# A planned schedule with larger GpSimd costs, margins for side matmuls, and parameters loaded with x

## The chip, the cores and the metric

One core of one Trainium2 chip. The metric is device time in microseconds: 293.01 us before the change (median of three runs, 292.58 to 294.14).

## The reference, cut to what matters

Two layers over 256 tokens of width 1024, all in float32. Each layer normalises the stream, projects it once, splits the result over three groups of heads, gates each, joins them and projects back:

```python
for l in range(DEPTH):                                   # DEPTH = 2
    u = rms_norm(x, g_pre[l]) @ w_in[l]
    (qa, ka, va, ga, qb, kb, vb, gb, rb, qm, gm) = jnp.split(u, split_idx, axis=-1)
    oa = moba_attention(norm(qa), norm(ka), va) * silu(ga)          # 8 heads, causal, ALiBi
    log_a = log_sigmoid(rb @ w_gate_up[l] + b_gate_up[l]) / 16
    ob = rms_norm(gla_attention(qb, kb, vb, log_a)) * silu(gb)      # 4 heads, gated linear, chunks of 64
    mk, mv = jnp.split(rms_norm(mem, g_mem[l]) @ w_mem_kv[l], 2, axis=-1)
    om = mem_attention(norm(qm), norm(mk), mv) * silu(gm)           # 4 heads into 256 memory tokens
    x = x + jnp.concatenate([oa, ob, om], axis=-1) @ w_out[l]
```

## The kernel before, in words

**Projections.** The stream lies transposed on chip (`xT`, eight k blocks of 128 x 256). Weights come in granules of 1024 x 256, 1 MB each, on SyncE's queue into three buffers (`raw`). To multiply float32 exactly enough, every operand is split into a high and a low part: ScalarE copies to the high part (`whi`, L380), VectorE subtracts for the low part (`wlo`, L382), and each product is three matmuls (L974; L981 where two granules are done side by side with 512 columns). A layer has 19 granules, 48 matmuls each; they are issued by `main()` in the order of `UNITS`, the granule gb and four output granules o0 to o3 last. The first output granule goes over k in the order of `KORD` (6, 7, 1, 0, 2, ...), two matmul groups per k. These are the projections; all the other matmuls are called side matmuls here: sums of squares (L414), the row form of the scale (L431), transposes of the normalised heads (L478), the low-rank gate (L499, L506), gated linear attention (L655 to L723), attention scores (L856), transposes of the probabilities (L908) and their product with the values (L923). Those of 64, 32 or 16 rows or columns are "tiled".

**Other engines.** GpSimd does the powers of -1/2 for the norms (L421 with 2, L458 with 8 elements a partition), the scaling of the probabilities (L893), copies of q with the heads kept apart (L534), and a share of the copies for which the planner may choose (L249: `xh`, `oh`, `zl`, `qsh`). L465 applies the norm to the heads, L708 is the product of gated linear attention, fed by copies into `att`. `put_o` (L826, L828) splits a finished head pair for the output projection.

**The planner.** No engine's order is written out by hand. Everything is a generator that yields operations to `Plan`, each with an engine (or several to choose from), a cost in nanoseconds and a time at which its inputs are ready. `Plan.run` picks again and again the operation that can start first, on the alternative that ends first; among operations of that engine that could start by then the highest priority goes. It writes the instruction there and books the engine. Projections have priority 0, side work 5 to 10. So costs and ready times decide the order of instructions and who does a copy; the hardware then runs each engine's queue in that order, waiting on semaphores. `begin` adds the cost of changing TensorE between full and tiled shape (`ENTER`, `LEAVE`, `CROSS`). `LANDS` are the planned landing times of the first chunks. GpSimd's costs: `gcost` for scaled copies and powers written in place:

```python
def gcost(n, scalar=False):
    return 330 + 0.83 * n if scalar else 75 + 2.42 * n
...
t1 = yield op("G", 800, t, 9)
G.tensor_tensor(r, v, nhalf[:, 0:2], op=ALU.pow)
...
t = yield op("G", 1620, t, prio)
G.tensor_tensor(c, ss, nhalf, op=ALU.pow)
```

**The start.** `start_loads` sends the parameters (`prm`: gains and biases, 46 floats a partition, 23 KB) on ScalarE's queue first, then an activation that brings in the exp table, then the first two weight chunks of kq; x, the first granule vr and the rest of kq go on SyncE's queue in five steps of k. The first scaling of x (L247) needs x and the parameters.

Of the kernel before, what the change touches and what calls it, by code (L numbers as in the profile page):

```python
# [16 lines left out]
P = 128  # L17
L = 2
KT = 8
T = 256  # L20
EPS = 1e-6
NPRM = 23
# [8 lines left out]
MEMPRIO = 6  # L31
WARM = 6
CHUNKS = ((0, 1), (1, 2), (2, 4), (4, 6), (6, 8))
LANDS = ((3400, 4800, 5300), (5300, 5700, 5800), (6600, 7200, 7900), (8600, 9300, 10000), (10600, 11300, 12000))
ENTER, LEAVE, CROSS = 89.0, 189.0, 60.0
C_ID = 0
C_MASK = 128
C_DIAG = 128 + 80
# [4 lines left out]
class Plan:  # L43
# [10 lines left out]
    def spawn(self, gen, prio=0):  # L54
        self.ready.append(Task(gen, prio))

    def begin(self, t, eng):
        s = max(t.after, self.free[eng])
        if eng == "P" and t.mode != self.shape:
            s += ENTER if self.shape == "full" else LEAVE if t.mode == "full" else CROSS  # L60
        return s

    def run(self):
        while True:
            while self.ready:
                self.step(self.ready.pop(0))
            if not self.pending:
                return
            best, pick = None, {}
            for t in self.pending:  # L70
                s, eng, cost = min(((self.begin(t, e), e, c) for e, c in t.alts), key=lambda a: a[0] + a[2])
                pick[t] = (s, eng, cost)
                key = (s, -t.prio, t.seq)
                if best is None or key < best[0]:
                    best = (key, eng)
            s, eng = best[0][0], best[1]
            t = min((t for t in self.pending if pick[t][1] == eng and max(t.after, self.free[eng]) <= s),
                    key=lambda t: (-t.prio, t.seq))
            s, _, cost = pick[t]
            self.pending.remove(t)  # L80
            if t.table and t.table != self.table:
                self.table = t.table
                cost += 1283.0
            self.free[eng] = s + cost
            if eng == "P":
                self.shape = t.mode
            t.value = s + cost + self.LAT[eng]
            if len(t.alts) > 1:
                t.value = (eng, t.value)
            self.step(t)  # L90
# [64 lines left out]


@with_exitstack
def trunk(ctx, tc, xT_d, memT_d, wvr_d, win_d, wmkv_d, wout_d, prm_d, wup_d, cst_d, nb_d, out_d):
    nc = tc.nc
    cp = ctx.enter_context(tc.tile_pool(name="cp", bufs=1))  # L160
    sp = ctx.enter_context(tc.tile_pool(name="sp", bufs=1))
# [9 lines left out]
    def big(shape, nm, dt=F32, parts=P):  # L171
        return cp.tile([parts] + shape, dt, name=nm)
# [4 lines left out]
    def ev():  # L177
        return Event(plan)

    xT = big([KT, T], "xT")  # L180
    xh, xl = big([KT, T], "xh", F32R), big([KT, T], "xl", F32R)
    oh, ol = big([KT, T], "oh", F32R), big([KT, T], "ol", F32R)
    prm, cst = big([L, NPRM], "prm"), big([N_CONST], "cst")
    wup = big([L, P], "wup", parts=16)
    nb = big([8, T], "nb")
    ident = cst[:, C_ID:C_ID + P]
# [46 lines left out]
        return (55 if psum else 95) + 0.83 * n + 93 * ptr  # L233

    def gcost(n, scalar=False):
        return 330 + 0.83 * n if scalar else 75 + 2.42 * n

    def copy(dst, src, n, psum, after, prio=None, scale=None, alts="SV"):
        costs = {"S": scost(n, psum, 0 if scale is None else 1),
# [66 lines left out]
        return t  # L306

    def start_loads():
        prm_t = 3550
        S.dma_start(prm, prm_d)  # L310
        S.activation(warm, ones, AF.Exp)
        tiles = []
        for i in range(2):
            l, nm, src, n = seq[i]
            got, t0 = yield ("acq", raws, 1)
            raw, src = sub(got[0][2], n), src.rearrange("p (k n) -> p k n", n=n)
            ts = [ev() for _ in range(KT)]
            tiles.append((raw, src, ts))
            plan.spawn(split(i, l, nm, n, got, ts, CHUNKS), 6)
        for (a, b), (tx, tv, tq) in zip(CHUNKS, LANDS):  # L320
            nc.sync.dma_start(xT[:, a:b], xT_d[:, a:b])
            plan.spawn(first_x(a, b, max(tx, prm_t)), 9)
            for (raw, src, ts), tw, q in zip(tiles, (tv, tq), (nc.sync, nc.scalar if b <= 2 else nc.sync)):
                q.dma_start(raw[:, a:b], src[:, a:b])
                for k in range(a, b):
                    ts[k].set(tw)
        plan.spawn(first_sq(tx), 5)
        nc.sync.dma_start(cst, cst_d)
        cst_ev.set(12300)
        nc.sync.dma_start(wup, wup_d)  # L330
# [78 lines left out]
    def stats(sq, t, out, Rout):  # L409
        got, t0 = yield ("acq", banks, 1)  # L410
        ps = got[0][2]
        t = yield op("P", 300, max(t, t0), 9)
        for tt in range(2):
            TE.matmul(ps[:, tt:tt + 1], lhsT=sq[0][2][:, tt * P:tt * P + P], rhs=ones, start=True, stop=True)  # L414
        sqsp.release(sq, t)
        v, e, r = (small([2], n) for n in ("vx", "evx", "rsx"))
        t = yield op("V", 80, t, 9)
        V.tensor_scalar(v, ps[:, 0:2], 1.0 / 1024, EPS, op0=ALU.mult, op1=ALU.add)
        banks.release(got, t)
        t1 = yield op("G", 800, t, 9)  # L420
        G.tensor_tensor(r, v, nhalf[:, 0:2], op=ALU.pow)  # L421
        t = yield op("V", 80, t, 9)
        V.tensor_scalar(e, v, EPS, None, op0=ALU.mult)
        out.set(t1, (r, e))
        if Rout is not None:
            got, t0 = yield ("acq", banks, 1)
            tc_ = yield ("wait", cst_ev)
            ps = got[0][2]
            t = yield op("P", 430, max(t1, t0, tc_), 9)
            for tt in range(2):  # L430
                TE.matmul(ps[:, tt * P:tt * P + P], lhsT=r[:, tt:tt + 1].to_broadcast([P, P]), rhs=ident,  # L431
                          start=True, stop=True)
            t = yield op("V", vcost(T), t, 9)
            V.tensor_copy(R_t, ps[:, :T])
            banks.release(got, t)
            Rout.set(t)

    def headnorm(parts, e, after_read, prio=None):
        got, t0 = yield ("acq", sqp, 1)
        sq = got[0][2]  # L440
        t = t0
        for ps, a, t1 in parts:
            n = ps.shape[1]
            t2 = yield op("S", scost(n * T, True), max(t1, t0), prio)
            S.activation(sq[:, a:a + n], ps, AF.Square, scale=0.125)
            t = max(t, t2)
        ss, c = small([8], "ss"), small([8], "cc")
        t = yield op("V", vcost(512), t, prio)
        V.tensor_reduce(ss, sq.rearrange("p t (h d) -> p (t h) d", d=64), axis=AX, op=ALU.add)
        sqp.release(got, t)  # L450
        t = yield op("V", 90, t, prio)
        if e is None:
            V.tensor_scalar(ss, ss, EPS, None, op0=ALU.add)
        else:
            s2 = ss.rearrange("p (t h) -> p t h", t=2)
            V.tensor_tensor(s2, s2, e[:, :, None].to_broadcast([P, 2, 4]), op=ALU.add)  # L456
        t = yield op("G", 1620, t, prio)
        G.tensor_tensor(c, ss, nhalf, op=ALU.pow)  # L458
        got, t0 = yield ("acq", nhp, 1)
        t = max(t, t0)  # L460
        for ps, a, _ in parts:
            n = ps.shape[1]
            v = ps.rearrange("p t (h d) -> p (t h) d", d=64)
            t = yield op("V", vcost(n * T), t, prio)
            V.tensor_tensor(got[0][2][:, a:a + n].rearrange("p t (h d) -> p (t h) d", d=64), v,  # L465
                            c[:, 4 * a:4 * a + 4 * n, None].to_broadcast([P, 4 * n, 64]), op=ALU.mult)
        after_read(t)
        return got, t
# [537 lines left out]
            wrel[l, nm][k // 2].set(t)  # L1006

    def main():
        yield op("P", 5400)
        for j in range(WARM):  # L1010
            TE.matmul(banks.slots[7][2][:, 0:256], lhsT=zero[:, 0:128], rhs=zero, start=True, stop=True)
        idx = {(l, n): i for i, (l, n, _, _) in enumerate(seq)}
        for l in range(L):
# [5 lines left out]
            for unit in UNITS[l] if l == 0 else ("vr", "kq", *UNITS[l]):  # L1019
# [15 lines left out]
                for k, m in order:  # L1035
# [3 lines left out]
                        tw = max(tw, tx)  # L1039
                    tx = yield ("wait", aev[k])  # L1040
                    if len(names) == 2:
                        t = yield op("P", 680, max(tb, tw, tx))
                        mms2(bk[m][2].rearrange("p (a n) -> p a n", a=2), act, k, m, k == 0, k == KT - 1)
                    else:
                        t = yield op("P", 360 * n / 256, max(tb, tw, tx))
                        ps = bk[m][2][:, :n] if nbk == 2 else bk[0][2][:, m * T:m * T + T]
                        mms(ps, l, kind, done[l, nm], act, k, m, k == 0, k == KT - 1)
                    ends[m] = t
# [28 lines left out]
            for g in range(4):  # L1077
# [16 lines left out]
                for k, m in order:  # L1094
                    tw = yield ("wait", wts[l, nm][k])
                    to = yield ("wait", oev[l][k])
                    w = done[l, nm]
                    t = yield op("P", 360, max(tb, tw, to))
                    ps = bk[m][2][:, :T]
                    mms(ps, l, "f", w, (oh, ol), k, m, k == KORD[l][0], k == KORD[l][-1])  # L1100
                    feed(l, nm, k, t)
# [4 lines left out]
    def first_unit():  # L1106
# [3 lines left out]
        for k in range(KT):  # L1110
            for nm, kind, bk, n in (("vr", "t", bv, 272), ("kq", "f", bq, T)):
                for m in range(2):
                    tw = yield ("wait", wts[0, nm][k])
                    tx = yield ("wait", xev[0][k])
                    t = yield op("P", 360 * n / 256, max(tw, tx))
                    mms(bk[m][2][:, :n], 0, kind, done[0, nm], (xh, xl), k, m, k == 0, k == KT - 1)
                    feed(0, nm, k, t)
                if k == KT - 1:
# [108 lines left out]
```

## Time and profile before

| | |
|---|---|
| median of three runs | 293.01 us |
| the profiled execution | 292.38 us, of which the span of the program's instructions is 290.6 us |
| TensorE busy (modelled) | 277.8 us, 96% |
| VectorE, ScalarE, GpSimd busy | 228.8, 189.2, 94.4 us |
| granted TensorE clock | full speed in all of the span |
| HBM read | 44.34 MB, 156 GB/s over the span |

A row of a timeline gives the start and duration in microseconds, the engine, the line, the operation, output <- inputs, and in brackets how long the engine had sat idle before it and on what it waited. Busy TensorE time overlaps from matmul to matmul, so starts tell more than durations.

### The profile page before, as it was taken

What the parts mean: (1) busy time and instruction counts of PE and PEld (TensorE: products, weight loads), DVE (VectorE), ACT (ScalarE), POOL (GpSimd) and SP (SyncE); (2) the same over time, 40 slices, a digit from 0 to 9 for tenths busy, and PEclk for the clock granted to TensorE, in tenths of its full rate; (3) what the DMA queues carried; (4) which work ended last, traced back from release to release, by engine and by line L of the source; (5) the groups of instructions that cost most, each with busy time, mean ns of one, the idle gap of its engine ahead of it and who ended that gap; (6) DMA issues with size and microseconds to landing.
All of it is one profiled execution on the core that took longest, in us unless ns stands there. A gap on an engine that the chain in (4) does not pass through costs nothing.

```text
span 290.6 us, 5785 instructions
## 1 busy us (share of the span) xinstructions
PE 277.8 (96%) x2140; PEld 244.7 (84%) x2140; DVE 228.8 (79%) x571; ACT 189.2 (65%) x420; POOL 94.4 (32%) x120
## 2 busy tenths in 40 slices
PE   8998998979899999999999999899999999999995
PEld 6798786748799979899999887579987778999995
DVE  2888599969979958987899679858997776979531
ACT  3766787637696957866774768658688565857410
POOL 3301392871450742400055037404052930600000
PEclk9999999999999999999999999999999999999999
DMA  6999607460532342046644743407341606143111
GB/s 177 306 358 391 248 2 289 153 280 3 203 126 108 106 187 111 36 145 202 242 147 144 284 152 114 178 0 289 114 178 26 266 12 280 18 142 133 54 54 38
DMA packets 9276, 45.76 MB, mean 157 GB/s; under 512 B 1168, under 2 KB 3104, under 8 KB 4256
## 3 DMA queue, kind: packets, MB, share of 16 engines
q1 hardware_dynamic: 8816, 45.10, 42.9%
q10 hardware_dynamic: 432, 0.29, 0.5%
q8 instruction: 17, 0.28, 0.4%
q14 instruction: 11, 0.09, 0.1%
HBM read 44.34 MB, written 1.05 MB: 156 GB/s over the span
## 4 chain that ended last, share of the span: by engine, by line
PE 64%; DVE 16%; DMA 6%; POOL 6%; ACT 5%; issue 2%; SPq 1%; DVEq 0%
PE bank L974 39%; PE bank L981 12%; DVE wlo L382 6%; PE bank L923 4%; PE bank L908 3%; POOL cc L458 3%; PE bank L856 3%; DMA raw<-win_dram 2%; DMA xT<-xT_dram 2%; POOL zl L249 2%; DMA raw<-wvr_dram 2%; ACT whi L380 2%; PE bank L478 1%; DVE acc L609 1%; PE bank L708 1%
## 5 line engine op out<-in xcount | busy, mean ns | idle before, releaser
L382 DVE TENSOR_TENSOR wlo<-raw,whi 128x512 fp32r<-128x512 f32 (+3 forms) x154 | 103.3, 693 | 16.5 <-ACT whi L380 14.1
L380 ACT ACTIVATE whi<-raw 128x512 fp32r<-128x512 f32 (+3 forms) x154 | 91.5, 620 | 30.2 <-PE bank L981 10.4
L974 PE MATMUL bank<-xh,whi 128*128 128x256 f32 x160 | 47.2, 295 | 0.0
L974 PE MATMUL bank<-xh,wlo 128*128 128x256 f32 x160 | 45.8, 286 | 0.6 <-DVE wlo L382 0.4
L974 PE MATMUL bank<-xl,whi 128*128 128x256 f32 x160 | 45.3, 283 | 0.0
L893 POOL TENSOR_SCALAR pe<-pe,rc 128x256 f32<-128x256 f32 (+1 forms) x48 | 29.1, 621 | 42.4 <-DVE rc L890 29.8
L974 PE MATMUL bank<-ol,whi 128*128 128x256 f32 x128 | 36.3, 284 | 0.0
L974 PE MATMUL bank<-oh,whi 128*128 128x256 f32 x128 | 36.3, 283 | 0.0
L974 PE MATMUL bank<-oh,wlo 128*128 128x256 f32 x128 | 36.3, 283 | 0.0
L981 PE MATMUL bank<-whi,xh 128*128 128x512 f32 x80 | 33.1, 414 | 0.0
L974 PEld LDWEIGHTS bank<-xh,whi 128*128 128x128 f32 x160 | 30.6, 191 | 1.4 <-issue 1.1
L974 PEld LDWEIGHTS bank<-xh,wlo 128*128 128x128 f32 x160 | 30.5, 191 | 1.1 <-DVE wlo L382 1.0
L981 PE MATMUL bank<-wlo,xh 128*128 128x512 f32 x80 | 31.4, 392 | 0.0
L981 PE MATMUL bank<-whi,xl 128*128 128x512 f32 x80 | 31.3, 391 | 0.0
L974 PEld LDWEIGHTS bank<-xl,whi 128*128 128x128 f32 x160 | 30.6, 191 | 0.0
L974 PE MATMUL bank<-whi,xh 128*128 128x256 f32 (+1 forms) x96 | 28.8, 300 | 0.2 <-ACT whi L380 0.2
L974 PE MATMUL bank<-wlo,xh 128*128 128x256 f32 (+1 forms) x96 | 27.8, 289 | 0.3 <-DVE wlo L382 0.2
L458 POOL TENSOR_TENSOR cc<-ss,nhalf 128x8 f32<-128x8 f32 x12 | 21.7, 1814 | 18.8 <-DVE ss L456 14.3
L974 PE MATMUL bank<-whi,xl 128*128 128x256 f32 (+1 forms) x96 | 27.3, 285 | 0.0
L974 PEld LDWEIGHTS bank<-ol,whi 128*128 128x128 f32 x128 | 24.6, 192 | 0.0
L974 PEld LDWEIGHTS bank<-oh,whi 128*128 128x128 f32 x128 | 24.6, 192 | 0.0
L974 PEld LDWEIGHTS bank<-oh,wlo 128*128 128x128 f32 x128 | 24.6, 192 | 0.0
(186 smaller groups left out, 598.0 us busy)
## 6 DMA issues: line engine op xcount, KB each, us to landing
raw<-win_dram SPq DMA_DIRECT2D x23, 1024.0 KB, 5.1
raw<-wout_dram SPq DMA_DIRECT2D x8, 1024.0 KB, 4.8
raw<-wmkv_dram SPq DMA_DIRECT2D x4, 1024.0 KB, 4.8
raw<-memT_dram SPq DMA_DIRECT2D x2, 1024.0 KB, 6.0
raw<-wvr_dram SPq DMA_DIRECT2D x1, 1088.0 KB, 5.0
nb<-nb_dram SPq DMA_DIRECT2D x1, 1024.0 KB, 10.3
out_dram<-xT SPq DMA_DIRECT2D x8, 128.0 KB, 1.9
raw<-wvr_dram SPq DMA_DIRECT2D x3, 272.0 KB, 5.3
```

The costliest lines, as they stand in the source:

```text
L249: G.tensor_scalar(dst, src, 1.0 if scale is None else scale, 1.0, op0=ALU.mult, op1=ALU.mult)
L380: S.activation(hi[:, cs], raw[:, cs], AF.Copy)
L382: V.tensor_sub(lo[:, cs], raw[:, cs], hi[:, cs].bitcast(F32))
L458: G.tensor_tensor(c, ss, nhalf, op=ALU.pow)
L478: TE.transpose(ps[:, m, tt * P:tt * P + P], n[:, tt, m * P:m * P + P], ident)
L609: V.copy_predicated(av, msk[:, None, mk:mk + 16].to_broadcast([P, 8, 16]).rearrange("p a (n t) -> p a n t", t=s), ps[:, a:a + P].rearrange ...
L856: TE.matmul(bk[hh][2][:, a:b], lhsT=x[ds], rhs=y[ds], start=(j == 0), stop=(j == len(prs) - 1))
L893: G.tensor_scalar(pe[:, hh, a:b], pe[:, hh, a:b], rc[:, hh, qt:qt + 1], 1.0, op0=ALU.mult, op1=ALU.mult)
L908: TE.transpose(bk[0][2][:, dst:dst + P], pe[:, hh, src:src + P], ident)
L923: TE.matmul(po[64 * hh:64 * hh + 64, q0:T], lhsT=vv[:, j, c:c + 64], rhs=pt[:, hh, 256 * j:256 * j + T - q0], start=(j == 0), stop=(j == 1))
L974: TE.matmul(ps, lhsT=a, rhs=b, start=(first and j == 0), stop=(lastk and j == 2))
L981: TE.matmul(ps, lhsT=a, rhs=b, start=(first and j == 0), stop=(lastk and j == 2))
```

## The change

Four things, in one edit. The planner's times for GpSimd are raised: powers from 800 and 1620 to 1300 and 2800 ns, scaled copies from 330 + 0.83 n to 450 + 1.5 n. A side matmul is planned no earlier than 300 ns after its inputs, a tiled one 600 ns later still while TensorE is in full shape; projections are marked "main" and have no such margin. The parameters lie ahead of x in one array, so the first x transfer brings them, and the activation with the table load is the first thing on ScalarE's queue. The planned landing times are set anew.

```diff
-LANDS = ((3400, 4800, 5300), (5300, 5700, 5800), (6600, 7200, 7900), (8600, 9300, 10000), (10600, 11300, 12000))
+LANDS = ((3600, 4300, 5000), (4600, 5200, 5600), (6100, 6800, 7500), (8200, 8900, 9600), (10300, 11000, 11700))
 ENTER, LEAVE, CROSS = 89.0, 189.0, 60.0
+SLACK, HOLD = 300.0, 600.0
...
+    def early(self, t, eng):
+        after = t.after
+        if eng == "P" and t.mode != "main":
+            after += SLACK + (HOLD if t.mode != "full" and self.shape == "full" else 0)
+        return max(after, self.free[eng])
+
     def begin(self, t, eng):
-        s = max(t.after, self.free[eng])
-        if eng == "P" and t.mode != self.shape:
-            s += ENTER if self.shape == "full" else LEAVE if t.mode == "full" else CROSS
+        s, mode = self.early(t, eng), "full" if t.mode == "main" else t.mode
+        if eng == "P" and mode != self.shape:
+            s += ENTER if self.shape == "full" else LEAVE if mode == "full" else CROSS
         return s
...
-            t = min((t for t in self.pending if pick[t][1] == eng and max(t.after, self.free[eng]) <= s),
+            t = min((t for t in self.pending if pick[t][1] == eng and self.early(t, eng) <= s),
                     key=lambda t: (-t.prio, t.seq))
...
-                self.shape = t.mode
+                self.shape = "full" if t.mode == "main" else t.mode
...
-    xT = big([KT, T], "xT")
+    xp = big([L * NPRM + KT * T], "xp")
+    xT = xp[:, L * NPRM:].rearrange("p (k t) -> p k t", t=T)
...
     def gcost(n, scalar=False):
-        return 330 + 0.83 * n if scalar else 75 + 2.42 * n
+        return 450 + 1.5 * n if scalar else 75 + 2.42 * n
...
-        prm_t = 3550
-        S.dma_start(prm, prm_d)
         S.activation(warm, ones, AF.Exp)
...
-            nc.sync.dma_start(xT[:, a:b], xT_d[:, a:b])
-            plan.spawn(first_x(a, b, max(tx, prm_t)), 9)
+            xs = slice(L * NPRM + a * T if a else 0, L * NPRM + b * T)
+            nc.sync.dma_start(xp[:, xs], xp_d[:, xs])
+            plan.spawn(first_x(a, b, tx), 9)
...
-        t1 = yield op("G", 800, t, 9)
+        t1 = yield op("G", 1300, t, 9)
         G.tensor_tensor(r, v, nhalf[:, 0:2], op=ALU.pow)
...
-        t = yield op("G", 1620, t, prio)
+        t = yield op("G", 2800, t, prio)
         G.tensor_tensor(c, ss, nhalf, op=ALU.pow)
...
-                        t = yield op("P", 680, max(tb, tw, tx))
+                        t = yield op("P", 680, max(tb, tw, tx), None, None, "main")
```

The other three `op("P", ...)` of the projections are marked "main" in the same way.

## Rows read from the trace of the kernel before

**Rows 1.** The page, busy us (share of the span) x instructions of each engine.

```profile
PE 277.8 (96%) x2140; PEld 244.7 (84%) x2140; DVE 228.8 (79%) x571; ACT 189.2 (65%) x420; POOL 94.4 (32%) x120
```

**Rows 2.** Stretches: length, busy PE, PEld, DVE, ACT, POOL; granted clock, DMA share, GB/s.

```profile
20.00:110.00 90.00, 84.49 (x651) 71.11 (x650) 76.77 (x193) 64.50 (x142) 41.76 (x44) 1.00 0.48 178
110.00:154.00 44.00, 44.00 (x375) 42.68 (x374) 39.11 (x95) 31.37 (x72) 9.18 (x12) 1.00 0.43 149
154.00:200.00 46.00, 43.85 (x344) 35.99 (x344) 36.28 (x96) 29.60 (x58) 17.05 (x19) 1.00 0.40 150
```

**Rows 3.** Waits of TensorE: for whom, us in total, times, longest.

```profile
PE bank L478 <- DVE nh L465: 3.0, 3, 1.6
PE bank L414 <- DVE sqs L304: 1.9, 2, 1.1
PE bank L708 <- DVE att L251: 1.3, 2, 0.9
...
PE bank L981 <- DVE wlo L382: 0.9, 2, 0.6
...
PE bank L908 <- POOL pe L893: 0.2, 1, 0.2
```

**Rows 4.** Timeline of TensorE, 59 to 70 us, layer 0.

```profile
61.16 0.65 PE L662 MATMUL bank<-zl,ee 128*64 128x256 f32 x4
63.42 0.33 PE L478 MATMUL bank<-cst,nh 128*128 128x128 f32 x1 [1.60 <-DVE nh L465]
63.95 0.55 PE L478 MATMUL bank<-cst,nh 128*128 128x128 f32 x3 [0.20 <-DVE nh L465]
...
66.29 0.47 PE L981 MATMUL bank<-whi,oh 128*128 128x512 f32 x1
...
68.00 0.39 PE L981 MATMUL bank<-wlo,oh 128*128 128x512 f32 x1
68.22 0.40 PE L981 MATMUL bank<-whi,ol 128*128 128x512 f32 x1
68.55 0.71 PE L856 MATMUL bank<-kfT,qfT 64*128 64x128 f32 x8
...
69.95 0.50 PE L981 MATMUL bank<-whi,oh 128*128 128x512 f32 x1
```

**Rows 5.** Timelines of VectorE and GpSimd, 59 to 67 us.

```profile
60.51 0.68 DVE L382 TENSOR_TENSOR wlo<-raw,whi 128x512 fp32r<-128x512 f32 x1
...
66.50 0.69 DVE L382 TENSOR_TENSOR wlo<-raw,whi 128x512 fp32r<-128x512 f32 x1
...
59.39 5.12 POOL L458 TENSOR_TENSOR cc<-ss,nhalf 128x8 f32<-128x8 f32 x2 [1.01 <-DVE ss L456]
```

**Rows 6.** Timelines of GpSimd and TensorE, 176 to 184 us, layer 1.

```profile
176.03 5.74 POOL L249 TENSOR_SCALAR zl<-wz,cst 128x256 f32<-128x256 f32 x5 [5.82 <-DVE wz L640]
...
183.94 0.88 PE L478 MATMUL bank<-cst,nh 128*128 128x128 f32 x4 [1.23 <-DVE nh L465]
```

**Rows 7.** L458: ns min/median/max. Then a group of copies: busy us, mean ns.

```profile
L458 POOL TENSOR_TENSOR cc<-ss,nhalf x12: 1629/1644/3517, 59.4 to 228.3; 128x8 f32<-128x8 f32 x12
...
L249 POOL TENSOR_SCALAR zl<-wz,cst 128x256 f32<-128x256 f32 x4 | 5.9, 1491 | 12.0 <-DVE wz L640 12.0
```

**Rows 8.** Chain that ended last (start, us, what), and VectorE's timeline at 125 us.

```profile
123.37 30.22 PE bank L974 x249
256.52 30.80 PE bank L974 x255
...
124.99 0.42 DVE L828 TENSOR_TENSOR ol<-of,oh 128x256 fp32r<-128x256 f32 x1
```

**Rows 9.** The start: ScalarE's first scaling; DMA issues (KB, us to landing).

```profile
4.49 0.51 ACT L247 ACTIVATE xh<-xT,prm 128x256 fp32r<-128x256 f32 x1 [1.84 <-DMA prm<-prm_dram]
...
prm<-prm_dram ACTq DMA_DIRECT2D x1, 23.0 KB, 3.8
xT<-xT_dram SPq DMA_DIRECT2D x2, 128.0 KB, 4.3
...
DMA to landing us min/median/max: 3.6/5.1/6.0
```

More of the change, by code (lines that the diff above doesn't have):

```diff
@@ L157, in trunk @@
 @with_exitstack
-def trunk(ctx, tc, xT_d, memT_d, wvr_d, win_d, wmkv_d, wout_d, prm_d, wup_d, cst_d, nb_d, out_d):
+def trunk(ctx, tc, xp_d, memT_d, wvr_d, win_d, wmkv_d, wout_d, wup_d, cst_d, nb_d, out_d):
     nc = tc.nc
@@ L178, in ev @@
         return Event(plan)
-    xT = big([KT, T], "xT")
+    xp = big([L * NPRM + KT * T], "xp")
+    xT = xp[:, L * NPRM:].rearrange("p (k t) -> p k t", t=T)
     xh, xl = big([KT, T], "xh", F32R), big([KT, T], "xl", F32R)
     oh, ol = big([KT, T], "oh", F32R), big([KT, T], "ol", F32R)
-    prm, cst = big([L, NPRM], "prm"), big([N_CONST], "cst")
+    prm, cst = xp[:, :L * NPRM].rearrange("p (l n) -> p l n", n=NPRM), big([N_CONST], "cst")
     wup = big([L, P], "wup", parts=16)
@@ L1008, in main @@
     def main():
-        yield op("P", 5400)
+        yield op("P", 5400, 0.0, None, None, "main")
         for j in range(WARM):
@@ L1041, in main @@
                     if len(names) == 2:
-                        t = yield op("P", 680, max(tb, tw, tx))
+                        t = yield op("P", 680, max(tb, tw, tx), None, None, "main")
                         mms2(bk[m][2].rearrange("p (a n) -> p a n", a=2), act, k, m, k == 0, k == KT - 1)
                     else:
-                        t = yield op("P", 360 * n / 256, max(tb, tw, tx))
+                        t = yield op("P", 360 * n / 256, max(tb, tw, tx), None, None, "main")
                         ps = bk[m][2][:, :n] if nbk == 2 else bk[0][2][:, m * T:m * T + T]
@@ L1097, in main @@
                     w = done[l, nm]
-                    t = yield op("P", 360, max(tb, tw, to))
+                    t = yield op("P", 360, max(tb, tw, to), None, None, "main")
                     ps = bk[m][2][:, :T]
@@ L1114, in first_unit @@
                     tx = yield ("wait", xev[0][k])
-                    t = yield op("P", 360 * n / 256, max(tw, tx))
+                    t = yield op("P", 360 * n / 256, max(tw, tx), None, None, "main")
                     mms(bk[m][2][:, :n], 0, kind, done[0, nm], (xh, xl), k, m, k == 0, k == KT - 1)
@@ L1215 @@
     nc = bacc.Bacc("TRN2", target_bir_lowering=False, num_devices=1, dynamic_dma_scratch_size=1024)
-    arrays = {"xT_dram": fm(a["x"]), "memT_dram": fm(a["mem"]), "wvr_dram": wvr, "win_dram": win,
-              "wmkv_dram": wmkv, "wout_dram": wout, "prm_dram": prm, "wup_dram": wup, "cst_dram": cst,
+    xp = np.concatenate([prm.reshape(P, L * NPRM), fm(a["x"]).reshape(P, KT * T)], axis=1)
+    arrays = {"xp_dram": xp, "memT_dram": fm(a["mem"]), "wvr_dram": wvr, "win_dram": win,
+              "wmkv_dram": wmkv, "wout_dram": wout, "wup_dram": wup, "cst_dram": cst,
               "nb_dram": nb}
```

## The prediction

> **What bounds the kernel now.** I read the busy table first: TensorE is busy 277.8 us of a 290.6 us span [rows 1]. That figure is modelled, so next I cut the span into stretches [rows 2]. [...] From 110 to 154 us TensorE has no idle time at all; from 20 to 110 it lacks 5.5 us (90.00 less 84.49) and from 154 to 200 2.2 us (46.00 less 43.85). The change can win only in those two stretches and at the start. What the idle time waits for stands in TensorE's list of waits [rows 3]: 3.0 us for the normalised heads of L465 at the transposes of L478, 1.9 us for the sums of squares at the small matmuls of L414, 1.3 us for copies into the score tile at L708, and 0.9 us in which the projections themselves wait for split weights (L382). All but the last are side matmuls: an instruction that is not ready stands at the head of a queue that runs in the order written, and the projection matmuls behind it wait with it.
>
> [Rows 4] show the largest. Four matmuls of L662 start at 61.16; the next, a transpose, sits idle 1.60 us, its follower 0.20, and the projections (L981) return only at 66.29. They then run until 68.22 with no wait. VectorE wrote no split weights from the end of the one at 60.51 until the one at 66.50 [rows 5], so most of those projections could have run in the gap: it is bad order, not lack of work. The late input is GpSimd's: two powers (L458) took 5.12 us from 59.39 [rows 5], 2.56 each, where the planner reckons 1.62. In layer 1 the same thing: five scaled copies on GpSimd take 5.74 us, 1.15 each where the planner has 0.54 to 0.65, the power is queued behind them, and the transposes wait 1.23 us [rows 6].
>
> **The change part by part.** The sum is made against the profiled execution, 292.38 us; the median shown is 293.01, 0.63 above it, and I carry that over at the end.
>
> *Longer GpSimd times.* They add no instruction; they change the planner's order and who does a copy. A power goes from 1.62 to 2.80 us. Most of the twelve were well planned already (median 1644 ns, maximum 3517, [rows 7]); the pair at 59.39 now has 5.60 planned for 5.12 real. So the transposes are put later and projections ahead of them. I take the whole 3.0 us of [rows 3]: at 61 us the projections to fill it are shown. Bounds 0 (the waits turn up elsewhere) to -3.0. In [rows 7] the copies whose mean is 1491 ns are the ones most underrated (0.54 planned); with 0.83 the planner gives more of them to ScalarE, which has 25.5 us free between 20 and 110 us [rows 2]. If that cover fails, weight splits on ScalarE slip and the projections wait for L382; the nearest row is the 0.9 us of [rows 3].
>
> [...]
>
> *Margins.* Every side matmul is planned 0.3 us after its input, and a tiled one 0.9 us while TensorE is in full shape. Queued behind each are projections, which now go first. L708 waits 1.3 us in two pieces, the longer 0.9 [rows 3]: a margin of 0.9 covers both, -1.3 (bounds 0 to -1.3). L414 is not tiled and gets 0.3 against waits of 1.1 and 0.8: -0.6 (bounds 0 to -1.9, all of it). The wait of 0.2 at L908 goes: -0.2. Tiled matmuls that become ready within 0.9 us of each other now share a visit. A visit costs the change of shape: [rows 4] have 0.33 us from the start of the last projection at 68.22 to L856 where the projection before took 0.22 of the queue (68.00 to 68.22), and a first projection of 0.50 afterwards against 0.40, so about 0.2 to 0.3. By my count of the trace there are 24 such visits, from L506 at 31.78 us to L923 at 255.65; I take two merged, -0.6. Bounds: six merged, -1.8, or three more, +0.9.
>
> *What the margins delay.* Each round of attention has four steps on TensorE (scores, two transposes, product), so it comes 0.3 + 0.9 + 0.3 + 0.9 = 2.4 us later, and nothing is lost as long as projections remain. Layer 0's last side matmuls end at 123.37; then 249 projections run without a break [rows 8], 0.121 us each. Of these 240 are gb and the four output granules, so gb begins 9 later, at 124.5, and the first output granule 48 after that, at 130.3. It reads the last attention heads after four earlier k, 24 matmuls, at 133.2. They were ready at 125.4 [rows 8]: 7.8 us of slack, of which about 4 goes because the projections run ahead by what was saved. A delay of 2.4 fits: 0. In layer 1 255 projections follow [rows 8], six more, so 0.7 us more slack.
>
> *Parameters with x, table load first.* The first scaling of x waits 1.84 us, until 4.49, for the parameters [rows 9], which take 3.8 us to land; the quickest x chunk takes 3.6. One transfer of 151 KB takes the place of 23 and 128 KB, and ScalarE's queue loses one issue. The parameters' queue on ScalarE then holds only two weight chunks; SP's queue has no issue added. The scaling can start at 4.3 at best, -0.2, but the wider rows of the first chunk may take it back, and the next chunks arrive when they did. I take -0.2, between +0.3 and -0.8 (half of the 1.84 wait is about the most that earlier landing could give). The table load runs while ScalarE idles for that transfer: 0.
>
> *The new order's own errors.* All of the order after the first microseconds is made anew, and projections keep no margin. I add +0.9, the projections' own wait of [rows 3] once more (bounds 0 to +1.8, twice).
>
> Sum: -3.0 - 1.3 - 0.6 - 0.2 - 0.6 - 0.2 + 0.9 = -5.0, so 287.4 beside 292.38, and **288.0** beside the median. All bounds at once: -9.0 (284.0) and +3.0 (296.0).
>
> **Rivals.** *More than that.* The projections that run ahead release weight buffers sooner, the splits follow, and the 0.9 us of waits for L382 go too, with all of L414 and more merged visits: the sum at its low end, about 284. Against it: VectorE is busy 76.77 of 90 us in the stretch [rows 2] and splits are its largest work. Chance 0.10.
>
> *The waits only move.* GpSimd's times swing from 1.6 to 3.5 us for one instruction [rows 7], so a fixed time is too long for most and too short for a few; other side matmuls then stand at the head, and side work stretched by 1.2 us per power holds PSUM banks longer. The waits of [rows 3] stay but for L708 and the start: -1.5 + 1.8, about 293. [...] For it: most powers were planned rightly before. Against: main work to fill in is shown. Chance 0.16.
>
> *The side chain comes too late* (the one on the other side). Not 2.4 but three rounds' delay adds up, because the attention rounds share two buffers of each kind and a round starts when the one before it has ended: 7.2 us, and with the longer planned powers some 10. From about 4 us on (7.8 less what was saved) in layer 0, each microsecond is TensorE idling at the first output granule. 10 us would cost 6 there and 3 in layer 1 (8.5 of slack less 1.6 saved in that layer): 288.0 + 9, 297; the decision point against the time before is 5 us of such idling. For it: before, the last side matmuls end only 1.1 us ahead of gb's first. Against: the last round also starts when its own projections (qa1, ka1) end, and those come earlier. Chance 0.14.
>
> That the change does nothing is excluded for the order: 0.9 us is more than one projection step of 0.36 or 0.68, so tiled matmuls must move.
>
> **How the numbers follow.** A measurement of this kernel tells 0.5% from no change, 1.5 us: faster is below 291.5, slower above 294.5. The forecast has 0.60, its own range 285.5 to 291; with the first rival 0.70 is faster, 0.16 the same, 0.14 slower. The range from 284.0 to 294.5 leaves out the far end of the late side chain and a little at the bottom.
>
> **What would show it.** Right: TensorE's waits at L465's and L708's readers vanish from its list, the transposes after the powers sit behind more projections, fewer scaled copies on GpSimd and more on ScalarE, tiled visits fewer, TensorE without idle time from 110 us to the end of each layer. The first scaling waits for x alone, near 4.3 us. Wrong: idle time at the first output granule, released by L828 (late side chain); waits of projections for L382 above 2 us (splits now limit); or powers of 3 us and more with transposes still waiting behind them.

## The result, and the profile after

281.0 us (median of four, 280.91 to 284.32) against 292.92: ratio 0.961, 95% interval 0.954 to 0.969. The forecast was 288.0, with a range of 284.0 to 294.5; the sign was right, the size was not, and the time lies below the range. The first profiled execution of the changed kernel was its longest, 284.32 us, with a stretch at half TensorE clock (granted 0.50 from 54 to 57 us); so the rows here are those of a second profile, of 280.73 us (span 278.9), and the first comes in under the clock.

Lines moved by 7 to 13: L974, L981 (projections) are now L981, L988; L380, L382 are L387, L389; L414 is L421; L458, L465 are L465, L472; L478 is L485; L708 is L715. The page's busy and clock lines of the changed kernel (compare [rows 1]):

```profile
PE 272.3 (98%) x2140; PEld 240.9 (86%) x2140; DVE 228.6 (82%) x572; ACT 191.9 (69%) x429; POOL 90.0 (32%) x110
...
PEclk9999999999999999999999999999999999999999
```

Stretches of the same kernel, columns as in [rows 2]:

```profile
20.00:110.00 90.00, 88.05 (x702) 75.08 (x701) 80.15 (x203) 68.47 (x151) 39.27 (x41) 1.00 0.48 184
110.00:154.00 44.00, 43.92 (x374) 42.35 (x373) 39.30 (x99) 31.37 (x75) 10.95 (x14) 1.00 0.44 150
154.00:200.00 46.00, 45.89 (x379) 38.89 (x379) 41.12 (x99) 36.20 (x68) 15.71 (x13) 1.00 0.48 180
```

Idle time is down from 5.5 to 1.95 us and from 2.2 to 0.1: that is 5.6 us of the 11.7 by which the span fell. TensorE's waits (compare [rows 3]); those for nh have shrunk from 3.0 to 0.3, that at the product of linear attention is gone, and so is that at the transposes of the probabilities:

```profile
PE bank L421 <- DVE sqs L312: 1.1, 2, 0.6
PE bank L988 <- DVE wlo L389: 0.5, 1, 0.5
PE bank L485 <- DVE nh L472: 0.3, 1, 0.3
```

Where TensorE had stood idle for 1.60 us [rows 4], the transposes now come behind projections. Timelines of GpSimd, VectorE and TensorE of the changed kernel:

```profile
54.47 5.93 POOL L465 TENSOR_TENSOR cc<-ss,nhalf 128x8 f32<-128x8 f32 x2 [0.98 <-DVE ss L463]
...
54.80 1.88 DVE L389 TENSOR_TENSOR wlo<-raw,whi 128x512 fp32r<-128x512 f32 x3
...
59.79 0.60 PE L485 MATMUL bank<-cst,nh 128*128 128x128 f32 x4
...
62.94 0.66 PE L485 MATMUL bank<-cst,nh 128*128 128x128 f32 x4 [0.29 <-DVE nh L472]
```

The pair of powers got slower, 5.93 us where 5.60 was planned, and TensorE still waits only 0.29 us. It ran beside a row of VectorE subtractions; the three at 54.80 took 0.63 us each, no more than the single ones of [rows 5] (0.68, 0.69). Why a power takes 1.63 us at one time and up to 4.33 at another (L465 in this profile), no run here tells.

**An account of the whole span.** From the starts on TensorE's queue the span splits without rest into the time to the first projection, projection to projection, visits to side matmuls (from the last projection before to the first after), and the tail. I worked this out from every start in the two traces:

| us | before | after | difference |
|---|---|---|---|
| to the first projection | 5.42 | 5.60 | +0.18 |
| projection to projection | 216.29 | 211.09 | -5.19 |
| of that, idle before them | 1.95 | 0.63 | -1.32 |
| visits to side matmuls (59 and 56) | 65.32 | 58.71 | -6.62 |
| of that, idle in them | 6.37 | 1.57 | -4.80 |
| tail | 3.57 | 3.45 | -0.12 |
| span | 290.60 | 278.85 | -11.75 |

So 4.8 us are side waits, as forecast; 1.8 are visits made shorter otherwise, 1.3 are waits of the projections, and 3.9 are in the pace of projections that wait for nothing, which no step of the forecast had.

The first 120 of these steps have no side matmul among them, so they can be set apart as the start. The 121st projection starts at 23.19 us before and at 21.24 after. Of these 1.95 us, 1.03 are waits, 1.10 are in the pace (short waits can hide there, since busy TensorE time overlaps from matmul to matmul: at 58.65 us a projection of 512 columns is busy for 0.39 us, and the next starts after 0.22), and the first projection takes 0.18 back. Behind the 121st, the steps without their waits take 197.64 us before and 194.87 after: 2.8 of the 3.9 us of pace. The waits there fall by 0.3.

### The profile page after: what moved, and what is told of

The parts are those of the page before. It is cut to its first block, busy times and chain, and to the rows that moved or that the text cites. A ratio compares the mean times of both kernels' runs of the same rounds, so it can differ in the third digit from the quotient of the medians.

```text
span 282.5 us, 5777 instructions
## 1 busy us (share of the span) xinstructions
PE 274.9 (97%) x2140; PEld 243.3 (86%) x2140; DVE 229.2 (81%) x572; ACT 192.1 (68%) x429; POOL 87.3 (31%) x110
## 2 busy tenths in 40 slices
DMA packets 9132, 45.76 MB, mean 162 GB/s; under 512 B 1024, under 2 KB 2960, under 8 KB 4112
## 4 chain that ended last, share of the span: by engine, by line
PE 77%; DVE 11%; DMA 6%; ACT 2%; issue 2%; SPq 0%; DVEq 0%; ACTq 0%
PE bank L981 39%; PE bank L988 22%; DMA raw<-win_dram 5%; DVE wlo L389 4%; PE bank L863 3%; PE bank L930 3%; PE bank L915 3%; PE bank L485 2%; DMA xp<-xp_dram 2%; DVE ol L296 1%; ACT whi L387 1%; DVE sqs L312 1%; PE bank L715 1%; PE bank L604 1%; PE bank L662 1%
## 5 line engine op out<-in xcount | busy, mean ns | idle before, releaser
L389 DVE TENSOR_TENSOR wlo<-raw,whi 128x512 fp32r<-128x512 f32 (+3 forms) x154 | 104.3, 697 | 16.7 <-ACT whi L387 14.8
L387 ACT ACTIVATE whi<-raw 128x512 fp32r<-128x512 f32 (+3 forms) x154 | 91.5, 620 | 29.5 <-PE bank L988 7.5
L981 PE MATMUL bank<-xh,whi 128*128 128x256 f32 x160 | 46.7, 292 | 0.0
L981 PE MATMUL bank<-xh,wlo 128*128 128x256 f32 x160 | 44.9, 281 | 0.1
L981 PE MATMUL bank<-xl,whi 128*128 128x256 f32 x160 | 44.6, 279 | 0.0
L981 PE MATMUL bank<-oh,whi 128*128 128x256 f32 x128 | 36.2, 283 | 0.0
L981 PE MATMUL bank<-ol,whi 128*128 128x256 f32 x128 | 36.1, 282 | 0.1
L981 PE MATMUL bank<-oh,wlo 128*128 128x256 f32 x128 | 35.9, 281 | 0.0
L465 POOL TENSOR_TENSOR cc<-ss,nhalf 128x8 f32<-128x8 f32 x12 | 22.2, 1858 | 36.7 <-DVE ss L463 32.1
L988 PE MATMUL bank<-whi,xh 128*128 128x512 f32 x80 | 33.2, 415 | 0.0
L981 PEld LDWEIGHTS bank<-xh,whi 128*128 128x128 f32 x160 | 30.2, 188 | 1.5 <-issue 1.1
L988 PE MATMUL bank<-whi,xl 128*128 128x512 f32 x80 | 31.4, 393 | 0.0
L988 PE MATMUL bank<-wlo,xh 128*128 128x512 f32 x80 | 31.3, 391 | 0.0
L981 PEld LDWEIGHTS bank<-xh,wlo 128*128 128x128 f32 x160 | 30.2, 189 | 0.6 <-DVE wlo L389 0.5
L981 PEld LDWEIGHTS bank<-xl,whi 128*128 128x128 f32 x160 | 30.1, 188 | 0.1
L981 PE MATMUL bank<-whi,xh 128*128 128x256 f32 (+1 forms) x96 | 28.4, 295 | 0.0
L981 PE MATMUL bank<-wlo,xh 128*128 128x256 f32 (+1 forms) x96 | 27.3, 285 | 0.0
L981 PE MATMUL bank<-whi,xl 128*128 128x256 f32 (+1 forms) x96 | 27.1, 282 | 0.0
L981 PEld LDWEIGHTS bank<-oh,whi 128*128 128x128 f32 x128 | 24.5, 192 | 0.2 <-issue 0.2
L981 PEld LDWEIGHTS bank<-ol,whi 128*128 128x128 f32 x128 | 24.0, 188 | 0.3 <-DVE ol L835 0.3
L981 PEld LDWEIGHTS bank<-oh,wlo 128*128 128x128 f32 x128 | 24.0, 188 | 0.0
```

The lines of the kernel that those rows point to most:

```text
L387: S.activation(hi[:, cs], raw[:, cs], AF.Copy)
L389: V.tensor_sub(lo[:, cs], raw[:, cs], hi[:, cs].bitcast(F32))
L981: TE.matmul(ps, lhsT=a, rhs=b, start=(first and j == 0), stop=(lastk and j == 2))
L988: TE.matmul(ps, lhsT=a, rhs=b, start=(first and j == 0), stop=(lastk and j == 2))
```

## Experiments

### Where the operands lie

The pace of the projections had gone from 120 to 117 ns (median start to start at 256 columns). Packing the parameters with x moves xh, xl, oh and ol up by 184 bytes in every partition, while the weights stay. One line of the kernel before does that alone:

```diff
+    prm = big([L, NPRM], "prm")
     xT = big([KT, T], "xT")
-    prm, cst = big([L, NPRM], "prm"), big([N_CONST], "cst")
+    cst = big([N_CONST], "cst")
```

> The kernel before with one line moved: the parameters' tile is placed ahead of xT, so xT, xh, xl, oh and ol lie 184 bytes further up in every partition, as in the changed kernel; the order of instructions and all else stays. Theory 'order' (the 12 us come from the planner's new order alone): 293 us as before, projections still 120 ns apart. Theory 'place' (part of it comes from where the operands lie): projections of 256 columns go from 120 to 118 ns and in some units to 113 as in the changed kernel, and the time falls by 2 to 5 us, to 288 to 291.

291.15 us, ratio 0.9935 (0.990 to 0.997). The chain of waits has the same 255 projections at its end as [rows 8]:

```profile
254.61 30.24 PE bank L975 x255
```

118.6 ns each, before 120.8: the pace came as theory 'place' had it, and the time is just outside its range. In the account of this profile the steps behind the 121st projection take 194.96 us without their waits, as in the changed kernel (194.87; before 197.64); a first projection 0.7 us later and visits 0.4 us longer take part of it back. The reverse, the changed kernel with the places of before (xp allocated last, a hole of 184 bytes where the parameters were; the order of instructions is untouched):

> The changed kernel, its order untouched, with xh, xl, oh and ol put back to the places they had before relative to all other tiles. Theory 'place': pitch 120 ns again and 283 to 285 us. Theory 'order': 281 us, no difference.

283.42 us, 2.4 above the changed kernel, pitch 120 again, and 197.62 us for the steps behind the 121st projection. So by the medians the place is worth 1.5 us on the old order and 2.4 on the new, and by the pace 2.7 on either. Then the changed kernel with unused bytes behind ol:

```diff
+    pad = big([24], "pad")      # 96 bytes; then 256, 128 and 232 floats
```

> The changed kernel with 96 unused bytes behind ol, which takes back about half of the 184 by which xh, xl, oh and ol moved towards the weights. If the pitch of projections follows the distance evenly: 118 to 119 ns and 282 us. If it goes by some finer grid: 113 to 120 ns, with 280 to 283.5 us. The order of instructions is the changed kernel's.

> The changed kernel with 1024 unused bytes behind ol. If only the distance within 1024 bytes counts, the pitch stays at 117 ns with 113 in places and the time at 281; if the distance itself counts, the pitch goes to 120 or elsewhere and the time to 279 to 284.

> The changed kernel with 512 unused bytes behind ol. 1024 bytes left the pitch as it was, 96 raised it for 512 columns from 229 to 234 ns. If the grid is 512 bytes or finer by halves: pitch 117 and 229, 281 us. If it is 1024: another pair of pitches, 279 to 285 us.

> The changed kernel with 928 unused bytes behind ol, on a grid of 1024 the same as moving on by another 96 in the change's own direction. If the pitch of 256 columns falls further with the distance: below 117 ns and 278 to 280 us, the fastest version. If the changed kernel's place is already a good one of the grid: 281 to 284.

They gave 284.51, 281.64, 281.17 and 282.08 us. The last 222 projections in the chains of the changed kernel, and then with the old places, 96 and 512 bytes:

```profile
249.34 26.35 PE bank L981 x222
```

```profile
251.06 26.83 PE bank L982 x222
```

```profile
251.23 26.84 PE bank L982 x222
```

```profile
250.30 26.36 PE bank L982 x222
```

118.7, 120.9, 120.9 and 118.7 ns. 512 and 1024 bytes change nothing beyond the spread of the executions, 96 does (284.51 us, above both theories). These distances fit a pattern that repeats at 512 bytes or a part of it; why the place counts, no run here tells. It differs by shape: with 512 columns the old place is the better one (227 against 229 ns, median start to start in the profile of before and in the first of the changed kernel), and 96 and 928 bytes are the worst: 66 such projections in a row, with the old places and then with 96 and 928 bytes, are 227, 234 and 233 ns apart,

```profile
157.80 14.99 PE bank L989 x66
```

```profile
157.19 15.45 PE bank L989 x66
```

```profile
157.34 15.40 PE bank L989 x66
```

None beat the changed kernel.

### Each part alone

The longer GpSimd times alone, on the kernel before:

```diff
-        return 330 + 0.83 * n if scalar else 75 + 2.42 * n
+        return 450 + 1.5 * n if scalar else 75 + 2.42 * n
...
-        t1 = yield op("G", 800, t, 9)
+        t1 = yield op("G", 1300, t, 9)
...
-        t = yield op("G", 1620, t, prio)
+        t = yield op("G", 2800, t, prio)
```

> The kernel before with the three raised GpSimd times and nothing else. If the GpSimd times carry the gain: 288 to 290, TensorE's wait for nh at the transposes near 0, L708's wait of 1.3 us still there. If the margins carry it: 291 to 293.

288.39 us (0.983, 0.979 to 0.988). That is 4.3 us where the forecast had 3.0 for this part. The waits for nh are gone from TensorE's list and the two main others stand, as the forecast's step had it:

```profile
PE bank L414 <- DVE sqs L304: 1.5, 2, 1.2
...
PE bank L708 <- DVE att L251: 1.1, 2, 0.6
```

The margins alone: SLACK, HOLD, the method `early` and the "main" marks of the changed kernel put into the kernel before.

> The kernel before with the margins (300 ns for side matmuls, 600 more for tiled ones) and nothing else. If the margins carry the gain, 286 to 288 and the waits for nh at L478's transposes shrink; if the GpSimd times carry it, 291 to 293 with the waits for nh still above 2 us. Either way pitch 120 ns, as the tiles lie where they did.

291.98 us: 0.998, 0.995 to 1.0005, no difference that can be told. The waits at side matmuls did shrink, those for nh too (3.0 to 0.4, which neither theory had beside this time), but waits of the projections themselves came up:

```profile
PE bank L988 <- DVE wlo L389: 3.3, 1, 3.3
...
PE bank L988 <- ACT whi L387: 0.8, 1, 0.8
```

The start alone: the kernel before with everything of the changed one but its GpSimd times, and with

```diff
-SLACK, HOLD = 300.0, 600.0
+SLACK, HOLD = 0.0, 0.0
```

> The changed kernel with both margins at 0 and GpSimd's old times: what is left is the start (parameters with x, table load first, new landing times) and the places of the tiles. If the start adds nothing to the place of the tiles: 291 us (layout alone gave 291.15). If the earlier first scaling (3.1 us instead of 4.5 in the changed kernel) is worth what it shows: 289 to 290.

287.23 us (0.981, 0.976 to 0.986), 5.5 below the kernel before and well under what either theory gave. In its profile the account gives 1.6 us before the 121st projection (21.62), 1.9 of pace behind it, 3.2 of visits (51 where there were 59), and 1.2 more waits of the projections. The place explains 1.5 to 1.9 of it; the visits are the planner's order.

### TensorE's clock

What the margins alone lose is seen in two stretches, around those waits and behind them (the clock is the column after POOL):

```profile
50.00:56.00 6.00, 1.87 (x9) 1.04 (x7) 6.00 (x18) 6.00 (x15) 5.20 (x5) 0.91 0.60 191
56.00:62.00 6.00, 5.75 (x14) 4.55 (x15) 4.16 (x14) 1.08 (x3) 3.34 (x2) 0.52 0.88 328
```

From 50 to 56 us TensorE worked 1.87 us of 6.00; then it ran six microseconds at a granted 0.52, nearly all of them at 0.50, and did, by my estimate, the work of about three (0.52 x 5.75): its projections of 512 columns start 0.43 us apart there, 0.23 at 50 us. The first profiled execution of the changed kernel has 1.99 us idle at a side matmul, behind which the clock holds 1.00,

```profile
26.94 0.61 PE L421 MATMUL bank<-ones,sqs 128*128 128x1 f32 x4 [1.99 <-DVE sqs L312]
```

and around 52 us two short waits, behind which it falls:

```profile
51.11 0.60 PE L421 MATMUL bank<-ones,sqs 128*128 128x1 f32 x4 [0.63 <-DVE sqs L312]
...
53.27 0.53 PE L988 MATMUL bank<-wlo,oh 128*128 128x512 f32 x1 [0.51 <-DVE wlo L389]
...
54.00:57.00 3.00, 3.00 (x8) 2.30 (x7) 3.00 (x9) 2.19 (x5) 2.01 (x3) 0.50 0.51 210
```

The same kernel again tells whether that stretch belongs to it:

> [...]

280.95 us median, and no such stretch in the profile, although TensorE idles at the same two places for as long:

```profile
48.81 0.60 PE L421 MATMUL bank<-ones,sqs 128*128 128x1 f32 x4 [0.65 <-DVE sqs L312]
...
50.97 0.50 PE L988 MATMUL bank<-wlo,oh 128*128 128x512 f32 x1 [0.51 <-DVE wlo L389]
```

So these two waits alone don't decide it. Nor does the stretch alone explain the 284.32 us: another of the first four executions has the same mean clock, 0.994, and took 281.05. The mean granted clock of every execution is in its result, so this can be followed through all eight combinations of the three parts.

### The parts two by two

> The kernel before with margins and GpSimd times, the old start and the old places. If the parts add: 292.7 - 0.7 - 4.3 = 287.7. [...]

> The changed kernel with GpSimd's old times. If the parts add: 281 + 4.3 = 285.3. [...]

> The changed kernel with both margins at 0: the start, the places and GpSimd's longer times. If the parts add (288.4 with GpSimd's times alone, 287.2 with the start alone): 282.9, so that the margins are worth 1.9 us on top. If the margins matter only beside the longer times: 284 to 286, with the waits for att at L715 and for sums of squares above 2 us together.

Each is one kernel with the edits above in or out: margins and GpSimd times on the old start 287.11 us, margins and new start 286.10, GpSimd times and new start 287.28 (284.23 to 289.69; 286.79 without the longest). The first is near its sum (287.7), but the clock fell in three of its four executions; the second is 0.8 above its sum (285.3), with waits for wlo of 1.2 and for whi of 1.4 us; the third is above both of its theories. The last column below is an estimate of mine, the median of time less (1 - clock) x span: the time if the clock had held, with TensorE taken as busy all through.

| start, margins, GpSimd times | median us | clock of its executions | at full clock |
|---|---|---|---|
| old, none, old (28 executions beside the others) | 292.7 | 0.992 to 1.000 | 291.7 |
| old, margins, old | 292.0 | 0.987 to 0.992 | 288.7 |
| old, none, longer | 288.4 | 0.998 to 1.000 | 288.1 |
| old, margins, longer | 287.1 | 0.988 to 1.000 | 285.6 |
| new, none, old | 287.2 | 0.992 to 1.000 | 285.9 |
| new, none, longer | 287.3 | 0.988 to 1.000 | 285.4 |
| new, margins, old | 286.1 | 0.982 to 0.988 | 282.4 |
| all three (8 executions) | 281.0 | 0.994 to 1.000 | 280.6 |

By the medians the parts don't add at all: the margins are worth 0.7 us alone and 6.3 on top of the other two; the longer times 4.3 alone, nothing with the new start, 5.1 with start and margins. By the last column they come nearer to it, 12.4 us for the three alone against 11.1 together, though each still swings: margins 3.0 alone and 4.8 with both others; longer times 3.6, and 3.1, 0.5 and 1.8 beside margins, start and both; start 5.8, 2.7, 6.3 and 5.0 (alone, with the longer times, with the margins, with both). So by this estimate part of the odd pattern is clock: every execution with margins and the old GpSimd times (10 on the old start, 4 on the new) lost some of it, while the changed kernel loses it in 3 of 8. The correction is rough. For the kernel before it can be tried: its 14 executions at 0.999 or more have a median of 292.2 us, the 14 at 0.994 or less 293.1, which is 0.9 apart where the estimate takes off 1.7. The margins alone are thus worth something between 0.7 and 3.0 us; which, is not shown.

### The start, taken apart

The parameters sent as a transfer of their own again:

```diff
+        S.dma_start(xp[:, :L * NPRM], xp_d[:, :L * NPRM])
         S.activation(warm, ones, AF.Exp)
...
-            xs = slice(L * NPRM + a * T if a else 0, L * NPRM + b * T)
+            xs = slice(L * NPRM + a * T, L * NPRM + b * T)
```

> The changed kernel, order and places untouched, but the parameters come again in a transfer of their own, first on ScalarE's queue. If the transfer itself is worth something: the first scaling goes back from 3.1 to 4.5 us, the first unit of 96 projections ends 0.5 to 1 us later and the time is 281.5 to 282.5. If the planner's order is all that counts at the start: 281.

281.04 us: a transfer less is worth nothing. But the first scaling did not go back; it came at 3.14 us, with both transfers in by 3.12, so this run doesn't undo the earlier arrival. It is not the packing that brings it: all fifteen profiles with the new array have the first scaling at 2.92 to 3.14 us, the five with the old ones at 3.74 to 4.49 ([rows 9] are the latest). What else does is not taken apart; that a partition's row of the new array is 8376 bytes long in memory, where that of x was 8192, is one difference.

What the earlier arrival can do is seen on SyncE's queue. In the kernel before, eight transfers go out on the two queues together; the ninth, SyncE's sixth, waits until the parameters have landed. Here the same transfer waits for them too, but goes out at 3.13; in the changed kernel it is the eighth and waits for none. SyncE's wait and issue before, and the issue in the changed kernel:

```profile
SPq L324 <- DMA prm<-prm_dram: 1.5, 1, 1.5
...
4.49 0.33 SPq L324 DMA_DIRECT2D raw<-wvr_dram  x1
```

```profile
3.06 0.43 SPq L331 DMA_DIRECT2D raw<-wvr_dram  x1
```

The last chunk of kq lands at 15.13 us before, at 13.87 in the changed kernel and at 13.56 with the parameters apart. The 121st projection starts at 22.60 to 24.03 us in the five profiles with the old start and at 21.16 to 21.96 in the fifteen with the new one, 21.21 with the parameters apart and 21.35 with the old landing times below. So the new start is worth one to two microseconds there, and neither the missing transfer nor the planned landing times are what brings them. That the earlier landing brings them fits these rows, but no run separates it from the plan without its wait for the parameters.

In the changed kernel ScalarE waits for the first weight chunk after the first scaling, and the first projection starts at 5.60 (5.42 before):

```profile
3.13 0.51 ACT L255 ACTIVATE xh<-xp 128x256 fp32r<-128x256 f32 x1 [0.92 <-DMA xp<-xp_dram]
4.89 0.43 ACT L387 ACTIVATE whi<-raw 128x272 fp32r<-128x272 f32 x1 [1.25 <-DMA raw<-wvr_dram]
```

The planned landing times of before:

```diff
-LANDS = ((3600, 4300, 5000), (4600, 5200, 5600), (6100, 6800, 7500), (8200, 8900, 9600), (10300, 11000, 11700))
+LANDS = ((3400, 4800, 5300), (5300, 5700, 5800), (6600, 7200, 7900), (8600, 9300, 10000), (10600, 11300, 12000))
```

> The changed kernel with the landing times planned before, the transfers as changed. If the new landing times matter by the order at the start: the first sums-of-squares matmul stands one projection group earlier and waits, the 144th projection is 0.5 to 2 us later, 282 to 284. If they don't: 281.

282.56 us (281.07 to 283.69), 1.6 above the changed kernel, of which 0.8 is clock by the estimate above (281.4 against 280.6). The planned landing times move no transfer; if they count, it is by the order they make. The first sums-of-squares matmul does not wait here, as the first theory had it to: visits hold 0.3 us of idle time (1.6 in the changed kernel), and the projections wait 2.1 (0.6).

### The size of the margins

```diff
-SLACK, HOLD = 300.0, 600.0
+SLACK, HOLD = 300.0, 0.0
```

> The changed kernel with the 300 ns margin and without the 600 ns for tiled matmuls. If holding back the tiled ones is most of the margins' worth, as forecast (1.3 us of L715's waits and 0.6 us of merged visits): 282 to 283, with L715's wait back at about 1 us. If it is the 300 ns that counts: 281.

289.55 us, above even the kernel with no margins (287.28); at full clock the estimates are 286.1 and 285.4, so by the estimate most of that is clock again, at 0.988 in three of four executions. Its waits:

```profile
PE bank L988 <- DVE wlo L389: 2.9, 2, 1.7
PE bank L421 <- DVE sqs L312: 2.7, 2, 1.8
PE bank L915 <- POOL pe L900: 1.7, 2, 1.2
...
PE bank L715 <- DVE att L259: 0.5, 1, 0.5
```

L715's wait, which was to come back, is small; the time is lost elsewhere, in an order that differs all over. Then SLACK alone, 250 and 350 in place of 300:

> The changed kernel with a margin of 250 ns in place of 300. Theory 'margin' (the gain of the combination belongs to margins of about this size): 281 us within 1. [...]

> The changed kernel with a margin of 350 ns. [...]

283.32 and 283.51 us, seven of the eight executions at 0.999 or more, so here it is not the clock. Neither is within 1 us of 281: 50 ns either way cost some 2.4 us, which belongs to this one order. But both stay 8.5 us or more below the kernel before (291.99 beside them), and that much belongs to the combination.

## Why the prediction was wrong

**Right: the side waits.** 3.0 + 1.3 + 0.6 + 0.2 = 5.1 us were to go and 4.8 did, all in the places named: nh 3.0 to 0.3, att 1.3 to 0, sums of squares 1.9 to 1.1. The last of these changes from execution to execution: eight profiles of this order have 0.5 to 2.6 us of side waits left, the first one 2.6 at the sums of squares alone. The longer GpSimd times alone cure the waits for nh and no other; but the margins alone shorten them to 0.4 as well, so which of the two did it in the whole change is not shown.

**Wrong: the first step and three terms.** The first step said that the change can win only where TensorE idles. It also won from projections that wait for nothing. The forecast's sum was -5.0 against a profiled execution; the account gives -11.75, so 6.7 us are missing, and they lie here:

- *The pace of projections that wait for nothing*, which had no term, measured -2.8 behind the 121st projection. "Parameters with x" was costed as a transfer and a few waits at the start; it also moves operands, and their place sets the pace of 1488 projections: 2.7 of the 2.8, by the runs on place alone. The forecast asked of each array when it arrives, not where it lies.
- *Parameters with x, table load first*, forecast -0.2 with bounds of +0.3 and -0.8, measured -1.95 at the 121st projection: 1.75 of the 6.7. The step that failed is "the next chunks arrive when they did". SyncE's sixth issue stood for 1.5 us until the parameters had landed; now it goes out 1.4 us sooner, and the last chunk of kq lands 1.3 us sooner. How much of the 1.95 this makes is open.
- *"The new order's own errors"*, forecast +0.9, measured -0.3 behind the 121st projection: 1.2 of the 6.7. The 0.9 was only the part of the projections' waits at L382 for two granules side by side; with those at L974 and the short ones it is 1.95 in all, over half of it at the start.
- *Merged visits*, forecast -0.6, measured -1.8 apart from idle time: 1.2 of the 6.7. Visits with a tiled matmul went from 26 to 24, so two merged, as forecast; what they saved was mis-sized. That the bound of six merged had just this size is luck.

Against this the side waits are 0.3 short of the forecast, and the tail 0.1 over it. The first rival's time, 284, was the nearest, at a chance of 0.10. Its reason, weight buffers that come free sooner, is not what is seen: of the 1.3 us by which the projections' waits fell, 1.0 lie in the first 120 steps.

The corners say the same from outside. On the new start alone 5.5 us go, and only 1.5 to 1.9 of that is place; the landing times, which I had not costed because they move no transfer, may be worth 0.8 to 1.6 in the changed kernel by the order alone, little more than the spread of the executions. The remainder of the start's worth (the table load, the plan without its wait for the parameters, the earlier arrival) was not taken apart.

**The granted clock,** 1.00 in [rows 2], had no term in the forecast. That was right for the profile read and not for the kernel: half of its executions ran at a mean of 0.994 or less, 0.9 us longer. That is little of the result, but by the estimate it hid part of the margins' worth when they stood alone.

**The late side chain** was rightly placed and came to its very edge. Its slack was over-read, though: the run of 249 projections does not hold all of gb but its last 30 matmuls, so the first output granule starts at 127.00 and not at 130.3, and the last heads, ready at 125.4, are needed behind five earlier k, at 130.72. Timeline of TensorE before:

```profile
127.00 0.28 PE L974 MATMUL bank<-oh,whi 128*128 128x256 f32 x1
...
130.72 0.28 PE L974 MATMUL bank<-ol,whi 128*128 128x256 f32 x1
```

That is 5.3 us of slack where the forecast had 7.8. Side work now ends later beside the projections: in layer 0, 204 projections follow the last side matmul, where 249 did, and the 14th of them starts as its operand is written. Chain of the changed kernel:

```profile
123.69 0.44 DVE ol L835
...
124.17 22.28 PE bank L981 x191
```

The heads come 1.3 us sooner than before, at 124.1, and are needed 6.5 us sooner, at 124.17: the 5.3 us of slack are used up, and that projection starts 0.38 us after the one before it where 0.12 is usual. The margins can hardly grow further without paying there.

**The second rival,** waits that only move, describes the margins alone: 4.1 us of waits at L988 where [rows 3] had 0.9 at the splits, and lost clock on top. In the whole change it did not come.

Left open: why the clock falls in some executions of an order and not in others. The half-clock stretches I read (granted 0.50) come within a few microseconds of idle time of TensorE around 25, 52 or 62 us; but the profile of before idles there too, 0.2 to 1.6 us at a time, and the second one of the changed kernel as long as the first; both hold 1.00.

## What to carry to other kernels

When a planner's numbers change, the whole order changes, and a part's worth depends on the others (0.7 us alone, 6.3 in company, by the medians): try combinations and neighbouring values, and look at the granted clock of every execution before calling a part worthless. After moving any array, compare the pace of instructions that wait for nothing, with the order unchanged if possible; a difference that is left may be the place of the operands, as it was here (120 to 117 ns, 2.7 us in all). Split a span by the starts on the bounding queue into pace, waits and visits before naming a cause: the sum must come out. At a start, follow which later transfer an early one holds back (here one was held for 1.5 us).

## What was not expected of the hardware

The pace of these matmuls changed with the place of their operands: 120 ns for 256 columns before, 117 after a move of 184 bytes (113 in some stretches of some executions), and 227 against 229 to 234 for 512 columns. TensorE fell to a granted clock of 0.50 for 3.4 or 6.8 us in the midst of the kernel, soon after idle times; eight of the twenty profiles have such a stretch, and one kernel with the same idle times has it in one execution and not in another. And the first x chunk and the parameters had landed by 3.14 us in every profile with the new array, in one transfer or two, where they took until 3.74 to 4.49 from arrays of their own.
